# One plain weight pair instead of two in the second feed-forward block, two products moved between its halves, and part of the low-order rests formed by GpSimd

## The chip, the cores and the metric

The kernel runs on one core of one Trainium2 chip. The metric is the device time of one launch in microseconds (us). The times given as "before" are the median of three runs; the profile is of one further execution. A core's engines are called here TensorE (PE in the profile, its weight loads PEld), VectorE (DVE), ScalarE (ACT), GpSimd (POOL) and SyncE (SP), which issues the DMAs.

## The reference

One encoder layer on x of 512 tokens by 1024 features, all in float32:

```python
def rmsnorm(x, g):
    y = x32 * lax.rsqrt(jnp.mean(x32 * x32, axis=-1, keepdims=True) + EPS)
    return (y * g).astype(x.dtype)

def swiglu(x, w_in, w_out):                    # w_in 1024 x 5632, w_out 2816 x 1024
    gate, up = jnp.split(x @ w_in, 2, axis=-1)
    return (jax.nn.silu(gate) * up) @ w_out

h = swiglu(rmsnorm(x, norm_ffn1_pre), w_ffn1_in, w_ffn1_out)
x = x + 0.5 * rmsnorm(h, norm_ffn1_post)
h = mixer(rmsnorm(x, norm_mix_pre), ...)       # gated convolution and mLSTM heads, not touched by the change
x = x + rmsnorm(h, norm_mix_post)
h = swiglu(rmsnorm(x, norm_ffn2_pre), w_ffn2_in, w_ffn2_out)
x = x + 0.5 * rmsnorm(h, norm_ffn2_post)
```

The two swiglu blocks ("block 1" and "block 2") are what the change touches.

## The kernel before, in words

**Numbers in two parts.** TensorE works on a rounded form of float32 (F32R). To keep float32 accuracy each operand is split in two: `split(hi, lo, src)` lets ScalarE copy `src` rounded into `hi` (a CAST, L292) and then lets another engine subtract, `lo = src - hi` (a TENSOR_TENSOR, L294). The second part is called the rest here. Its engine is the argument `eng`, VectorE by default. Each product is then three matmul groups, hi x hi, hi x rest, rest x hi. In the names, `whi`/`wlo` are the two parts of a weight, `big` a tile of x, of a left matrix or of the hidden h, `raw` a weight as loaded by DMA, `ps` a PSUM bank.

**A feed-forward block** (`ffn`) makes the 2816 hidden features in 22 pairs of weight tiles (a gate tile and an up tile of 1024 x 128 each). The 512 tokens are taken as two halves of 256.

- *Plain pairs* (`PLAIN = 2`, `plain`, L453): the first two pairs are multiplied directly, first all four tiles with the first half of the tokens, then all four with the second half. The second half needs the transposes of tile 3 of the normalised x (`flip_q(3, ...)`, L343), which in block 2 hang on the last step of the mixer's output: `between` puts them into the fourth tile's first half, before its last third. Their results are split into xq tiles.
- *Split pairs* (the other 20; `product`, `mm_part`, L431): gate and up are computed together by a seven-product scheme (of Strassen's kind, as a 2 x 2 by 2 x 2 product: features halved, tokens halved), each product 12 matmuls of 128x256. The combinations of x (T1 to T4) are formed once per block in `combine_x`; those of the weights in `w_pair`, which forms four sums and differences on VectorE (L158) and splits g, s1, c and u. Products 1 and 2 need the first token half only; all others need the second half or T1 to T4. VectorE then joins the products (L484 to L509), from PSUM.
- *The output product* takes h (features by tokens) times w_out. Ten of the 22 feature tiles, in five pairs, go through the same scheme in two passes: five a-steps (`left_a`, `w_out_a`: products 1, 5, 6, 7) and, after the sums of these are taken out of PSUM (`taken`, L574 and L576 on ScalarE, L531 on VectorE), five b-steps (`left_b`, `w_out_b`: products 2, 3, 4), all L564; the other features go directly (`mm_out`, L589). `left_a` splits three parts of the left matrix (256, 256 and 512 columns), `w_out_a` splits a tile of 1024 and two halves of 512, `w_out_b` one of 1024 and one of 512, into a tile called `wt`.

**Order.** Weights come by SyncE's DMA queue in the order of `stream`, through four `raw` buffers; split weights have twelve `w` buffers. The order of instructions on each engine is set at build time by a scheduler that works with its own estimates of duration; instructions passed to `pin` stay in program order, as long as `pinned` says so, and all others may move. Each engine then runs its queue strictly in that order. GpSimd forms the rests of the first four weight tiles of the kernel only (`ON_POOL`), beside small work of the norms (L310), masks and memsets.

Of the kernel before, what the change touches and what calls it, by code (L numbers as in the profile page):

```python
# [19 lines left out]
NT = S // P  # L20
KD = D // P
DFF = 2816
NF = DFF // P
# [7 lines left out]
WARM = 20  # L31
WARM2 = 4
ON_POOL = (0, 1, 2, 3)
PLAIN = 2


@with_exitstack
def encoder_kernel(ctx: ExitStack, tc: tile.TileContext, a: dict, out: bass.AP):
    nc = tc.nc
# [73 lines left out]
    for w_in, w_out in ((w1i, w1o), (w2i, w2o)):  # L113
        if w_in is w2i:
            stream += [cols(wm, c) for c in (Q0, Q0 + P, K0, K0 + P)]
            stream += [cols(wm, O0 + i * P) for i in range(4)]
            stream += [cols(wm, CG)]
            stream += [(wm[blk(i, 2 * P), V0:V0 + 512].rearrange("(k p) f -> p k f", p=P), 2) for i in range(4)]
            for i in range(4):
                stream += [cols(wm, c + i * P) for c in ((CG, HC, BG) if i else (HC, BG))]  # L120
            stream += [rows(wo, k * P) for k in MIXK[:5]]
        for j in range(NF):
            pair = [cols(w_in, j * P), cols(w_in, DFF + j * P)]
            stream += pair if j < PLAIN else [([v[0] for v in pair], KD)]
# [26 lines left out]
    def w_pair(g, u):  # L151
# [34 lines left out]
    def w_out_a(r0, r1):  # L186

        c = (slice(0, 512), slice(512, 1024))

        def sub(o, a_, b_):  # L190
            nc.vector.tensor_tensor(out=o, in0=a_, in1=b_, op=ALU.subtract)

        def wt(n):
            return wpool.tile([P, 1024], F32R, tag="w", name=nm(n))

        sub(r1[:, c[0]], r0[:, c[1]], r0[:, c[0]])
        sub(r0[:, c[1]], r1[:, c[1]], r0[:, c[1]])
# [156 lines left out]
    def combine_x(xq):  # L354
# [5 lines left out]
        def sub(o, a_, b_):  # L360
            nc.vector.tensor_tensor(out=o, in0=a_, in1=b_, op=ALU.subtract)

        def put(key, v):
            hi, lo = xq_hl(xq, key)
            split(hi, lo, v)

        v1, v3 = (t4().rearrange("p (k t) -> p k t", k=4) for _ in range(2))
        sub(v1, b12, b11)
# [1 line left out]
        sub(v3, b22, b12)  # L370
        sub(b22, b22, v1)
        put("t2", b22)
        put("t3", v3)
        sub(b21, b21, b22)
        put("t4", b21)

    def pre_norm(tb, g, parts=2):
        xs = t4()
# [53 lines left out]
                    o, ww[:, k, :], x[xx][:, k, :], start=first and n == 0, stop=n == 11, skip_group_check=True))  # L432
                n += 1

    def ffn(xq, between, finish, mid=None, within=None, ahead=(2, 2, 1, 1), late=None):

# [25 lines left out]
        pinned["rest"] = False  # L462
        if late:
            with tc.issue_after(mark["hi"].ins), tc.issue_after(mark["lo"].ins):
                w_split(1)
# [7 lines left out]


        h0, h1 = slice(0, 256), slice(256, 512)
        right = {1: (0, 0), 2: (1, 0), 3: (1, 1), 4: "t4", 5: "t1", 6: "t2", 7: "t3"}

        def product(n, w, o, first):
            mm_part(o[:, h0], w[n], xq_hl(xq, right[n]), first)

        def last(j, w, x, c, u):
            product(4, w, x, False)
# [4 lines left out]
        for j in range(PLAIN, NF):  # L487
            if j == PLAIN + 4 and late:
                late()
            w = w_get(1 if j < NF - 1 else 2)  # L490
            x, y, z = ps(), ps(), ps()
            a_, u, c = t2(), t2(), t2()
            product(1, w, x, True)
            pinned["PE"] = False
            nc.scalar.copy(a_[:, h0], x[:, h0])
            product(5, w, y, True)
# [43 lines left out]
        def left_a(i):  # L540
# [181 lines left out]
    def within1(tb):  # L722
# [9 lines left out]
        finish1, wgates, within1, (1, 1, 1, 0), late1)  # L732
    xT = st["xT"]


# [393 lines left out]
    def store(tb, h):  # L1129
        nc.sync.dma_start(out[0, blk(tb), h], x_t[tb][:, h])  # L1130

    ffn(xT3, {(3, 2): lambda: flip_q(3, xs[3], xT3)}, lambda tb, acc: post_norm(tb, acc, g_post3, 4.0, store, (1, 0) if tb == NT - 1 else (0, 1)))


_INS = [
# [26 lines left out]
```

## Time and profile before

| | before |
|---|---|
| runs | 918.28 us median of 3 (918.09 to 918.73) |
| the profiled execution | 915.36 us, span of its instructions 913.7 us |
| granted TensorE clock | 0.999 of full speed |
| VectorE, rests of 128x1024 (L294) | 197 from weights, 1218 ns mean |
| ScalarE, casts of 128x1024 (L292) | 211, 1028 ns mean |
| GpSimd, rests of 128x1024 (L294) | 4, 2402 ns mean |
| DMA | 96.47 MB, 106 GB/s mean |

Block 1 has its plain pairs until 36 us, its split pairs until 244, its output product from 228 to 353 us; then comes the mixer. Block 2 starts at 567.6 us, has its split pairs until 798 and its output product from 783 to 907 us. Rows of the timeline give the start and the length of an instruction or of several alike (xN), the engine, the line, and in brackets how long the engine had been idle and what ended that. "Busy" counts time in which at least one instruction of an engine runs; consecutive instructions overlap by some tens of ns, so that work on an engine is better counted by the distance of starts. Lines of helpers stand for many callers: L294 is every rest.

### The profile page before, as it was taken

The numbers are of one execution on the slowest core, as the hardware profiler recorded it, in microseconds if no ns is written. First come the engines' busy times: TensorE is split into PE (matmuls) and PEld (weight loads), VectorE is DVE, ScalarE is ACT, GpSimd is POOL, SyncE is SP. The second block draws the span as 40 slices with busy tenths as digits, with TensorE's granted clock in tenths as the row PEclk, the third lists the DMA queues.
The fourth block names the chain that finished last, engine by engine and source line by source line (L and its number), as shares of the span: only waits on it lengthen the run. The fifth ranks groups of instructions, "written<-read, shape, count | busy, mean of one in ns | idle before, by whom it ended". The sixth has DMA issues, their size and how long they took to land.

```text
span 913.7 us, 15022 instructions
## 1 busy us (share of the span) xinstructions
PE 900.1 (99%) x6015; PEld 816.7 (89%) x6015; DVE 716.2 (78%) x1196; ACT 444.6 (49%) x745; POOL 44.7 (5%) x67
## 2 busy tenths in 40 slices
PE   8999999999999999999999999999999999999997
PEld 7999999999877888987888888999999999977885
DVE  6988998888988359498787746889888988999435
ACT  6655555555456235452434335545545545566311
POOL 5000000000002001000011000000000000000000
PEclk9999999999999999999999999999999999999999
DMA  8233443343335614231422602224343432343402
GB/s 256 68 114 116 119 135 97 102 127 96 93 127 149 199 47 116 63 100 47 116 70 70 197 12 66 74 68 118 112 120 93 118 108 87 119 140 110 162 2 91
DMA packets 126257, 96.47 MB, mean 106 GB/s; under 512 B 4182, under 2 KB 114794, under 8 KB 126187
## 3 DMA queue, kind: packets, MB, share of 16 engines
q1 hardware_dynamic: 126186, 95.51, 35.1%
q8 instruction: 47, 0.77, 0.4%
q14 instruction: 24, 0.19, 0.1%
HBM read 93.40 MB, written 2.10 MB: 105 GB/s over the span
## 4 chain that ended last, share of the span: by engine, by line
PE 93%; DVE 4%; ACT 1%; issue 1%; DMA 1%; SPq 0%; POOL 0%; DVEq 0%; POOLq 0%; ACTq 0%
PE ps L431 43%; PE ps L589 13%; PE ps L422 12%; PE ps L564 9%; PE ps L453 5%; PE ps L1119 5%; PE ps L965 2%; DVE big L294 1%; DVE wlo L294 1%; PE ps L343 1%; DVE big L531 1%; PE ps L1035 1%; DMA x<-in_x_dram 1%; PE ps L983 0%; PE ps L391 0%
## 5 line engine op out<-in xcount | busy, mean ns | idle before, releaser
L294 DVE TENSOR_TENSOR wlo<-raw,whi 128x1024 fp32r<-128x1024 f32 x207 | 245.0, 1192 | 58.9 <-ACT whi L292 44.2
L292 ACT CAST whi<-raw 128x1024 fp32r<-128x1024 f32 x211 | 211.8, 1028 | 145.9 <-DVE raw L158 45.0
L431 PE MATMUL ps<-big,whi 128*128 128x256 f32 x1920 | 264.8, 280 | 0.0
L431 PEld LDWEIGHTS ps<-big,whi 128*128 128x128 f32 x1920 | 243.5, 188 | 0.5
L431 PE MATMUL ps<-big,wlo 128*128 128x256 f32 x960 | 150.9, 280 | 0.0
L431 PEld LDWEIGHTS ps<-big,wlo 128*128 128x128 f32 x960 | 129.3, 188 | 0.0
L589 PE MATMUL ps<-whi,big 128*128 128x512 f32 x384 | 121.9, 395 | 0.2 <-ACT whi L292 0.2
L589 PEld LDWEIGHTS ps<-whi,big 128*128 128x128 f32 x384 | 72.0, 188 | 17.4 <-ACT whi L292 0.6
L422 PE MATMUL ps<-big,whi 128*128 128x512 f32 (+1 forms) x384 | 79.8, 358 | 0.2 <-DVE den L1053 0.2
L564 PE MATMUL ps<-whi,big 128*128 128x512 f32 x240 | 75.9, 395 | 2.6 <-ACT big L292 2.6
L589 PE MATMUL ps<-wlo,big 128*128 128x512 f32 x192 | 75.6, 395 | 0.0
L422 PEld LDWEIGHTS ps<-big,whi 128*128 128x128 f32 x384 | 63.5, 188 | 11.2 <-PE ps L1077 0.4
L431 PE MATMUL ps<-big,ws 128*128 128x256 f32 x480 | 65.3, 280 | 0.0
L431 PEld LDWEIGHTS ps<-big,ws 128*128 128x128 f32 x480 | 60.3, 188 | 0.0
L564 PEld LDWEIGHTS ps<-whi,big 128*128 128x128 f32 x240 | 44.7, 188 | 13.4 <-ACT big L292 3.4
L501 ACT COPY t<-ps 128x256 f32<-128x256 f32 x40 | 14.9, 371 | 72.8 <-PE ps L431 72.7
L292 ACT CAST big<-big 128x512 fp32r<-128x512 f32 (+2 forms) x68 | 36.1, 582 | 23.2 <-DVE big L531 10.8
L564 PE MATMUL ps<-wlo,big 128*128 128x512 f32 x120 | 44.9, 393 | 0.0
L589 PEld LDWEIGHTS ps<-wlo,big 128*128 128x128 f32 x192 | 36.1, 188 | 8.4
L422 PE MATMUL ps<-big,wlo 128*128 128x512 f32 (+1 forms) x192 | 41.1, 356 | 0.0
L294 DVE TENSOR_TENSOR big<-big,big 128x512 fp32r<-128x512 f32 (+2 forms) x68 | 40.7, 634 | 0.1
L422 PEld LDWEIGHTS ps<-big,wlo 128*128 128x128 f32 x192 | 32.1, 188 | 5.5
(212 smaller groups left out, 1143.3 us busy)
## 6 DMA issues: line engine op xcount, KB each, us to landing
raw<-in_w_ffn_in_dram SPq DMA_DIRECT2D x88, 512.0 KB, 4.8
raw<-in_w_ffn_out_dram SPq DMA_DIRECT2D x44, 512.0 KB, 5.0
raw<-in_w_mix_in_dram SPq DMA_DIRECT2D x24, 512.0 KB, 4.5
raw<-in_w_mix_out_dram SPq DMA_DIRECT2D x8, 512.0 KB, 3.6
raw<-in_w_ffn_out_dram SPq DMA_DIRECT2D x10, 256.0 KB, 4.0
out_dram<-x SPq DMA_DIRECT2D x8, 256.0 KB, 2.0
x<-in_x_dram SPq DMA_DIRECT2D x4, 256.0 KB, 4.9
x<-in_x_dram SPq DMA_DIRECT2D x2, 512.0 KB
```

Of the source, the lines that this page charges most:

```text
L292: latest["hi"] = nc.scalar.copy(out=hi, in_=src)
L294: latest["lo"] = eng.tensor_tensor(out=lo, in0=src, in1=f32(hi), op=ALU.subtract)
L343: pin(nc.tensor.transpose(out=pt[:, blk(k)], in_=xs[:, blk(4 * b + k)], identity=ident))
L422: nc.tensor.matmul(o, ww[:, k, :], xk(xT, xx, k, sl), start=n == 0, stop=n == 3 * KD - 1)
L431: pin(nc.tensor.matmul(o, ww[:, k, :], x[xx][:, k, :], start=first and n == 0, stop=n == 11, skip_group_check=True))
L453: pin(nc.tensor.matmul(o, ww[:, k, :], xq_hl(xq, (k // 4, th))[xx][:, k % 4, :], start=n == 0, stop=n == 3 * KD - 1))
L501: nc.scalar.copy(a_[:, h1], x[:, h0])
L531: nc.vector.tensor_tensor(out=o, in0=a_, in1=b_, op=op)
L564: nc.tensor.matmul(acc[tb + t][half], left[n][x][:, blk(t)], right[n][y], start=first and x == y == 0, stop=last_ and x == 1, skip_group_c ...
L589: nc.tensor.matmul(acc[tb][half], hT[hh][:, blk(tb)], w[ww][:, blk(half, 512)], start=fresh and hh == ww == 0, stop=k == NF - 1 and hh == ...
L965: nc.tensor.matmul(pv_, xk(xT, xx, k, blk(tb)), ww[:, k % 2, :], start=n == 0, stop=n == 3 * KD - 1)
L1119: nc.tensor.matmul(acc[half], yy[yi][:, k % 4, blk(tb)], wmo[k][wi][:, blk(half, 512)], start=(n == 0 and yi == 0 and wi == 0), stop=(n == ...
```

## The change

Three things. `PLAIN` becomes an argument of `ffn`: block 1 keeps two plain pairs, block 2 gets one, and its second pair becomes a split pair. In block 2 products 1 and 2 of the first split pair are issued between the two token halves of the plain pair, followed by the transposes of tile 3 (`fill`); the loop then leaves these two out for that pair. And several calls of `split` get `nc.gpsimd` as the engine of the rest, in both blocks: u in `w_pair`, two halves in `w_out_a`, one in `w_out_b`, the 512 columns in `left_a`, T3 and T4.

```diff
-PLAIN = 2
...
-            stream += pair if j < PLAIN else [([v[0] for v in pair], KD)]
+            stream += pair if j < (2 if w_in is w1i else 1) else [([v[0] for v in pair], KD)]
...
         uh, ul = wt("whi"), wt("wlo")
-        split(uh, ul, u)
+        split(uh, ul, u, nc.gpsimd)
...
-        split(bh[:, c[0]], bl[:, c[0]], r1[:, c[0]])
-        split(bh[:, c[1]], bl[:, c[1]], t)
+        split(bh[:, c[0]], bl[:, c[0]], r1[:, c[0]], nc.gpsimd)
+        split(bh[:, c[1]], bl[:, c[1]], t, nc.gpsimd)
...
-        split(t[:, c[0]], t[:, c[1]], r1[:, c[0]])
+        split(t[:, c[0]], t[:, c[1]], r1[:, c[0]], nc.gpsimd)
...
-        put("t3", v3)
+        put("t3", v3, nc.gpsimd)
         sub(b21, b21, b22)
-        put("t4", b21)
+        put("t4", b21, nc.gpsimd)
...
-    def ffn(xq, between, finish, mid=None, within=None, ahead=(2, 2, 1, 1), late=None):
+    def ffn(xq, between, finish, PLAIN, mid=None, within=None, ahead=(1, 1), late=None, fill=None):
...
+        pre = None
+        if fill:
+            pre = w_get(0), ps(), ps()
+            product(1, pre[0], pre[1], True)
+            product(2, pre[0], pre[2], True)
+            fill()
...
+            ready_ = pre if j == PLAIN else None
+            w = w_get(1 if j < NF - 1 else 2) if not ready_ else pre[0]
+            x, y, z = (pre[1], ps(), pre[2]) if ready_ else (ps(), ps(), ps())
...
+            if ready_:
+                w_split(1)
+            else:
+                product(1, w, x, True)
...
-            product(2, w, z, True)
+            if not ready_:
+                product(2, w, z, True)
...
-            split(hi[:, 512:1024], lo[:, 512:1024], a_)
+            split(hi[:, 512:1024], lo[:, 512:1024], a_, nc.gpsimd)
...
-    ffn(xT3, {(3, 2): lambda: flip_q(3, xs[3], xT3)}, lambda tb, acc: post_norm(...))
+    ffn(xT3, {}, lambda tb, acc: post_norm(...), 1, fill=lambda: flip_q(3, xs[3], xT3))
```

How this stands on the engines, at three places. First TensorE at the start of block 2 (numbers are tiles; L343/L342 are the transposes of tile 3, L453 matmuls of plain pairs, L431/L430 of split pairs; big_5654 and big_5663 are x's first token half, big_5848 and big_5856 its second). Before:

```order
L453 MATMUL ps_6027<-big_5654,whi_5949 128x256 x4
L453 MATMUL ps_6027<-big_5663,whi_5949 128x256 x4
L343 MATMUL ps_6044<-ident,t_875_5883 128x128 x4
L453 MATMUL ps_6027<-big_5654,wlo_5950 128x256 x2
L343 MATMUL ps_6051<-ident,t_875_5883 128x128 x4
L453 MATMUL ps_6027<-big_5654,wlo_5950 128x256 x2
L453 MATMUL ps_6027<-big_5663,wlo_5950 128x256 x4
L431 MATMUL ps_6212<-big_5654,whi_6010 128x256 x8
L431 MATMUL ps_6212<-big_5654,wlo_6011 128x256 x4
L453 MATMUL ps_5922<-big_5848,whi_5906 128x256 x4
```

and after:

```order
L453 MATMUL ps_5965<-big_5663,wlo_5913 128x256 x4
L430 MATMUL ps_5990<-big_5654,whi_5948 128x256 x8
L430 MATMUL ps_5990<-big_5654,wlo_5949 128x256 x4
L430 MATMUL ps_5991<-big_5663,whi_5948 128x256 x8
L430 MATMUL ps_5991<-big_5663,wlo_5949 128x256 x4
L342 MATMUL ps_6016<-ident,t_875_5883 128x128 x4
L342 MATMUL ps_6023<-ident,t_875_5883 128x128 x4
L453 MATMUL ps_5916<-big_5848,whi_5906 128x256 x4
L453 MATMUL ps_5965<-big_5848,whi_5912 128x256 x4
L453 MATMUL ps_5916<-big_5856,whi_5906 128x256 x4
```

Both products now stand ahead of the transposes, and the second token half (big_5848) follows directly behind them, where eighteen matmuls of the first half and of product 1 stood between.

Second, GpSimd's queue in block 2. Before, the small steps of the norms (rs) of block 2's input and output follow each other directly:

```order
L310 TENSOR_TENSOR rs_5878<-rs_5876,nhalf 128x1
L310 TENSOR_TENSOR rs_5892<-rs_5890,nhalf 128x1
L310 TENSOR_TENSOR rs_9392<-rs_9390,nhalf 128x1
L310 TENSOR_TENSOR rs_9442<-rs_9440,nhalf 128x1
L310 TENSOR_TENSOR rs_9491<-rs_9489,nhalf 128x1
```

After, 43 rests stand there; these are the first ones (u of the first split pair, T3, T4, u of the next two):

```order
L309 TENSOR_TENSOR rs_5878<-rs_5876,nhalf 128x1
L309 TENSOR_TENSOR rs_5892<-rs_5890,nhalf 128x1
L293 TENSOR_TENSOR wlo_5962<-raw_5943,whi_5961 128x1024
L293 TENSOR_TENSOR big_6067<-t_911_6057,big_6067 128x4x256
L293 TENSOR_TENSOR big_6071<-big_5666,big_6071 128x4x256
L293 TENSOR_TENSOR wlo_6126<-raw_6107,whi_6125 128x1024
L293 TENSOR_TENSOR wlo_6206<-raw_6187,whi_6205 128x1024
```

In the second block's order they are 21 rests of u, T3 and T4, then 10 weight halves, 5 left halves and 5 of `wt`; in block 1 the same with 20 of u. All come from VectorE's queue.

Third, ScalarE where the a-steps end and the first b-step begins (COPY rows are `taken`; big_8919, then big_8929, is the first b-step's left matrix). Before:

```order
L574 COPY big_8668<-ps_8660 128x512
L574 COPY big_8668<-ps_8661 128x512
L576 COPY big_8668<-ps_8662 128x512
L576 COPY big_8668<-ps_8663 128x512
L292 CAST wt_8879<-raw_8875 128x512
L292 CAST whi_8927<-raw_8925 128x1024
L292 CAST big_8919<-big_5898 128x512
```

and after:

```order
L586 COPY big_8678<-ps_8670 128x512
L291 CAST wt_8889<-raw_8885 128x512
L291 CAST whi_8937<-raw_8935 128x1024
L586 COPY big_8678<-ps_8671 128x512
L291 CAST whi_8943<-raw_8941 128x1024
L588 COPY big_8678<-ps_8672 128x512
L588 COPY big_8678<-ps_8673 128x512
L291 CAST big_8929<-big_5898 128x512
```

The two weight casts moved ahead of the last copies, so that the left matrix's cast now follows the copies directly.

More of the change, by code (lines that the diff above doesn't have):

```diff
@@ L361, in sub, with put @@
             nc.vector.tensor_tensor(out=o, in0=a_, in1=b_, op=ALU.subtract)
-        def put(key, v):
+        def put(key, v, eng=nc.vector):
             hi, lo = xq_hl(xq, key)
-            split(hi, lo, v)
+            split(hi, lo, v, eng)
         v1, v3 = (t4().rearrange("p (k t) -> p k t", k=4) for _ in range(2))
@@ L462, in ffn, with product @@
         pinned["rest"] = False
+        right = {1: (0, 0), 2: (1, 0), 3: (1, 1), 4: "t4", 5: "t1", 6: "t2", 7: "t3"}
+        def product(n, w, o, first):
+            mm_part(o[:, slice(0, 256)], w[n], xq_hl(xq, right[n]), first)
+        pre = None
[4 more added lines that the diff above has]
+            fill()
         if late:
@@ L475, in ffn @@
         h0, h1 = slice(0, 256), slice(256, 512)
-        right = {1: (0, 0), 2: (1, 0), 3: (1, 1), 4: "t4", 5: "t1", 6: "t2", 7: "t3"}
-        def product(n, w, o, first):
-            mm_part(o[:, h0], w[n], xq_hl(xq, right[n]), first)
         def last(j, w, x, c, u):
@@ L489, in ffn @@
                 late()
-            w = w_get(1 if j < NF - 1 else 2)
-            x, y, z = ps(), ps(), ps()
+            ready_ = pre if j == PLAIN else None
+            w = w_get(1 if j < NF - 1 else 2) if not ready_ else pre[0]
+            x, y, z = (pre[1], ps(), pre[2]) if ready_ else (ps(), ps(), ps())
             a_, u, c = t2(), t2(), t2()
-            product(1, w, x, True)
+            if ready_:
+                w_split(1)
+            else:
+                product(1, w, x, True)
             pinned["PE"] = False
@@ L731, in encoder_kernel @@
         },
-        finish1, wgates, within1, (1, 1, 1, 0), late1)
+        finish1, 2, wgates, within1, (1, 1, 1, 0), late1)
     xT = st["xT"]
@@ L1130, in store @@
         nc.sync.dma_start(out[0, blk(tb), h], x_t[tb][:, h])
-    ffn(xT3, {(3, 2): lambda: flip_q(3, xs[3], xT3)}, lambda tb, acc: post_norm(tb, acc, g_post3, 4.0, store, (1, 0) if tb == NT - 1 else (0, 1)))
+    ffn(
+        xT3, {}, lambda tb, acc: post_norm(tb, acc, g_post3, 4.0, store, (1, 0) if tb == NT - 1 else (0, 1)), 1,
+        fill=lambda: flip_q(3, xs[3], xT3),
+    )
 _INS = [
```

## The prediction

> **What bounds the kernel now.** I read the page's busy times first, then the chain of waits, then busy times by stage.
>
> ```profile
> PE 900.1 (99%) x6015; PEld 816.7 (89%) x6015; DVE 716.2 (78%) x1196; ACT 444.6 (49%) x745; POOL 44.7 (5%) x67
> PE 93%; DVE 4%; ACT 1%; issue 1%; DMA 1%; SPq 0%; POOL 0%; DVEq 0%; POOLq 0%; ACTq 0%
> ```
>
> TensorE is busy 99% of the span and the chain that ends last is 93% TensorE: time falls only if TensorE gets less to do or waits less, and it rises if anything makes TensorE wait. GpSimd is nearly free, which is what the change draws on. The next rows (PE, PEld, DVE, ACT, POOL busy) show where another engine stands close behind.
>
> ```profile
> 60.00:225.00 165.00, 165.00 (x1404) 165.00 (x1403) 143.09 (x224) 88.84 (x139) 0.00 (x0) 1.00 0.40 114
> 225.00:258.00 33.00, 33.00 (x182) 28.46 (x182) 33.00 (x66) 16.45 (x32) 0.00 (x0) 1.00 0.44 131
> 560.00:610.00 50.00, 50.00 (x400) 48.68 (x399) 42.12 (x60) 28.24 (x44) 2.01 (x3) 1.00 0.29 85
> 610.00:776.00 166.00, 166.00 (x1412) 166.00 (x1412) 143.34 (x225) 85.63 (x136) 0.00 (x0) 1.00 0.37 107
> 776.00:815.00 39.00, 39.00 (x224) 33.94 (x223) 38.27 (x72) 21.82 (x41) 0.00 (x0) 1.00 0.43 132
> 815.00:836.00 21.00, 18.62 (x78) 14.23 (x77) 19.88 (x34) 15.68 (x29) 0.00 (x0) 1.00 0.26 73
> ```
>
> In the split-pair stages (60:225, 610:776) TensorE never stops and VectorE is busy 86%: it has 14% to spare. Where the pairs end and the five a-steps of the output product run (225:258, 776:815), VectorE is busy 33.00 of 33.00 and 38.27 of 39.00 us beside a TensorE that does not stop either: two bounds at once. Right behind it (815:836) TensorE loses 2.4 us.
>
> **The change, part by part.** *One plain pair becomes a split pair in block 2.* A plain pair is 4 x 24 = 96 matmuls of 128x256, a split pair 7 x 12 = 84.
>
> ```profile
> 567.59 2.04 PE L453 MATMUL ps<-big,whi 128*128 128x256 f32 x16
> 577.93 0.60 PE L343 MATMUL ps<-ident,t 128*128 128x128 f32 x4
> 579.75 1.09 PE L431 MATMUL ps<-big,whi 128*128 128x256 f32 x8
> 581.13 2.50 PE L453 MATMUL ps<-big,whi 128*128 128x256 f32 x20
> 592.40 1.58 PE L431 MATMUL ps<-big,ws 128*128 128x256 f32 x12
> 593.82 1.11 PE L431 MATMUL ps<-big,whi 128*128 128x256 f32 x8
> 574.54 1.42 DVE L383 SCALAR_TENSOR_TENSOR t<-x,rs,gb 128x512 f32<-128x512 f32 x2 [0.44 <-POOL rs L310]
> 578.57 1.26 ACT L292 CAST big<-ps 128x512 fp32r<-128x512 f32 x2 [3.38 <-PE ps L343]
> ```
>
> The 12 matmuls at 592.40 take until 593.82, so 0.118 us each: 12 fewer are **-1.4 us** (a split period is 84 x 0.118 = 9.9 us).
>
> *Fill.* Tile 3 is ready at 574.54 + 1.42 = 575.96 and its transposes now come at 577.93, behind 88 matmuls. Afterwards 48 + 24 = 72 matmuls stand ahead of them: 567.59 + 72 x 0.118 = 576.1, still 0.1 us behind the data. But behind them one product (579.75 to 581.13) covers the ScalarE copies today; afterwards the second halves follow at once. The first copy ends 578.57 + 0.63 = 579.2, 1.27 us after the transposes began; the eight transposes cover about 0.8. That leaves 0.5; with the margin of 0.1 I take **+0.6** (0.4 to 1.3, if VectorE is late with tile 3).
>
> *The rests on GpSimd.* The order counts, per block, 20 or 21 rests of u (128x1024), T3 and T4 (128x1024), and in the output product 10 weight halves, 5 left halves and 5 of the fourth factor (128x512).
>
> ```profile
> L294 POOL TENSOR_TENSOR wlo<-raw,whi 128x1024 fp32r<-128x1024 f32 x4 | 9.6, 2402 | 1.4 <-ACT whi L292 1.3
> 777.67 2.36 DVE L294 TENSOR_TENSOR wlo<-raw,whi 128x1024 fp32r<-128x1024 f32 x2
> 779.94 0.42 DVE L508 TENSOR_TENSOR t<-ps,t 128x256 f32<-128x256 f32 x1
> 781.75 0.69 DVE L294 TENSOR_TENSOR wlo<-raw,whi 128x512 fp32r<-128x512 f32 x1
> 782.35 0.69 DVE L294 TENSOR_TENSOR wlo<-t,whi 128x512 fp32r<-128x512 f32 x1
> ```
>
> On VectorE one of 1024 takes (779.94 - 777.67)/2 = 1.13 us, one of 512 0.60 (781.75 to 782.35). On GpSimd one of 1024 takes 2.40; for 512 there is no row, half is 1.20, an estimate. If the two engines ran side by side, this would be free. The rows say that they do not:
>
> ```profile
> L706 POOL CAST big<-rawg x4: 209/440/1207, 284.0 to 285.4; 128x32 fp32r<-128x32 f32 x4
> 284.18 1.24 DVE L294 TENSOR_TENSOR wlo<-raw,whi 128x1024 fp32r<-128x1024 f32 x1 [0.26 <-ACT whi L292]
> 285.35 1.31 DVE L294 TENSOR_TENSOR big<-big,big 128x512 fp32r<-128x512 f32 x2
> 458.25 0.64 POOL L1018 TENSOR_SCALAR_AFFINE_SELECT t<-t 128x512 f32<-128x512 f32 x1 [14.08 <-ACT t L1016]
> 458.47 0.96 DVE L294 TENSOR_TENSOR big<-t,big 128x512 fp32r<-128x512 f32 x1
> ```
>
> The same little GpSimd cast takes 0.209 at best and 1.207 beside VectorE's subtraction of two SBUF operands at 284.18: it finishes when that one does. The other way round, the subtraction at 458.47 overlaps a GpSimd instruction for 0.42 us and takes 0.96 instead of 0.69: 0.27 lost, two thirds of the overlap. (The four GpSimd splits that give the 2.40 ran beside VectorE instructions that read PSUM, so they show nothing of this.) Nearly all that VectorE does in these stages reads two SBUF operands. So a rest on GpSimd costs VectorE between 0 and its whole length; the nearest row gives two thirds: 1.60 for 1024 against 1.13 saved, 0.80 for 512 against 0.60 saved. VectorE would lose by the move.
>
> Where this lands: per split pair VectorE has 0.86 x 9.9 = 8.5 us; 8.5 - 1.13 + 1.60 = 9.0 (9.8 at full length) of 9.9, so TensorE keeps setting the pace: **0** in steady pairs. At each block's start T3, T4 and the first u come within some 20 us on a loaded VectorE: 3 x 0.47 = 1.4 (0 to 3 x 1.27 = 3.8), partly absorbed: **+1** per block. Block 2 also gets a split pair's VectorE work, 8.5 us, in place of a plain pair's two splits and one product, 2 x 1.13 + 0.60 = 2.9; of the 5.6 more, T3, T4 and the first u (3.4) leave VectorE, and the 7.9 us that VectorE idles in 560:610 cover the rest; if that cover is gone, it adds up to 2.2. In the a-steps VectorE has no time to spare: 15 halves x 0.20 + one u of 0.47 = 3.5, and each rest comes 0.6 later (1.20 - 0.60) plus up to one instruction of 0.60 that holds GpSimd up, 4.7 together. How much TensorE feels depends on VectorE's lead.
>
> ```profile
> 813.46 0.68 DVE L294 TENSOR_TENSOR big<-big,big 128x512 fp32r<-128x512 f32 x1
> 813.84 0.86 PE L564 MATMUL ps<-wlo,big 128*128 128x512 f32 x3
> ```
>
> In block 2 the last left rest ends at 814.14 while TensorE is in the matmuls of that step: no lead, **+4**. For block 1 I take the middle, **+2**. Bounds: 0, or 15 x 0.60 + 1.27 = 10.3 if all of GpSimd's time blocks VectorE.
>
> VectorE's in-place differences in the left matrices now also wait for GpSimd, with all of VectorE's queue behind them; this is inside the same bounds. On the DMA queue nothing moves but one gain load; its loads wait for GpSimd instead of VectorE to free u, at most 2.4 us later, and the rest of u is needed by the last products of a pair only: nothing.
>
> *ScalarE's order at the first b-step.*
>
> ```profile
> 814.97 1.08 ACT L576 COPY big<-ps 128x512 f32<-128x512 f32 x2 [0.33 <-PE ps L564]
> 816.45 1.06 ACT L292 CAST whi<-raw 128x1024 fp32r<-128x1024 f32 x1
> 817.40 1.97 ACT L292 CAST big<-big 128x512 fp32r<-128x512 f32 x4
> 818.08 0.50 PE L564 MATMUL ps<-whi,big 128*128 128x512 f32 x1 [1.28 <-ACT big L292]
> 263.27 0.50 PE L564 MATMUL ps<-whi,big 128*128 128x512 f32 x1 [1.28 <-ACT big L292]
> ```
>
> TensorE waits 1.28 us in each block for a cast that stands behind two weight casts, which the new order puts ahead of the last copies. Closed in both blocks it is -2.6; if VectorE is late already, nothing. I take **-1.3**.
>
> Sum: -1.4 + 0.6 + 1 + 1 + 2 + 4 - 1.3 = +5.9. The profiled execution took 915.36 (span 913.7) and would take 921.3; it lies 2.9 under the median of the runs, 918.28, which becomes **924.2**.
>
> **Rivals.** *VectorE's lead is enough (faster).* For: 14% to spare in the pairs. Against: none to spare at 776:815. It decides if a rest on GpSimd blocks VectorE for less than it saves, under 1.13 of 2.40. Then -1.4 + 0.6 - 2.6 = -3.4: 914.9.
>
> *The terms cancel (no change):* the a-steps cost 1 to 3 in all, 917 to 920.
>
> *Full blocking.* Each GpSimd rest holds VectorE for its whole length: (10.3 - 2 of lead) + 10.3 in the a-steps, 2 at each start, no gap closed: -0.8 + 18.6 + 4 = +21.8, 940. For: the casts at 284 waited for all of VectorE's instruction. Against: the row at 458.47, two thirds. The Trainium skill (SBUF — State Buffer, "Who interferes with whom") states this rule: VectorE with two SBUF inputs and a GpSimd instruction that reads SBUF exclude each other, and the later one blocks until the other is done. By that rule the sum would be this rival's; the trace agrees for GpSimd waiting (1.207 against 0.209) and shows VectorE waiting only once.
>
> **Chances.** Forecast (920.2 to 932) 0.45, full blocking 0.15, faster 0.26, cancelled 0.14. The bound of what can be told from no change is 0.2%, 1.8 us: faster 0.26, same 0.14, slower 0.60. The range 914.0 to 939 leaves out the lower fringe of the faster case and the upper half of full blocking; the forecast's own is 920.2 to 932.
>
> **What would show it.** VectorE's subtractions of 1024 lengthen from 1.22 where GpSimd runs, and GpSimd's from 2.40; TensorE's new idle time is named after L564's successors waiting for POOL or DVE rests around 225:260 and 775:820; the 1.28 waits shrink; the transposes of tile 3 start near 576 with about half a microsecond of wait behind them. I am wrong if VectorE's instructions keep their lengths beside GpSimd, or if the a-steps run without gaps.

## The result and the profile after

| | before | after |
|---|---|---|
| runs | 918.18 us median of 4 (917.49 to 918.73) | 952.93 us median of 4 (947.38 to 954.66) |
| ratio | | 1.0368 (95% interval 1.0326 to 1.0411) |
| profiled execution | 915.36 us, span 913.7 | 952.85 us, span 951.1 |
| granted TensorE clock | 0.999 | 0.989 |

The change makes the kernel 3.7% slower, about 34 us; the prediction said 924.2 (914.0 to 939.0). The direction was right, the size was not.

The page after, busy times and the chain of waits:

```profile
PE 914.1 (96%) x6003; PEld 823.6 (87%) x6003; DVE 746.3 (78%) x1121; ACT 447.1 (47%) x750; POOL 240.0 (25%) x152
PE 24%; DVE 4%; POOL 2%; ACT 1%; issue 1%; DVEq 0%; POOLq 0%; ACTq 0%
```

VectorE has 75 instructions fewer and is busy 30 us longer. TensorE has 12 matmuls fewer and is busy 14 us longer: part of the loss is a slower clock. Before, 93% of the span could be followed through TensorE; now the chain passes to and fro between the engines.

Busy times by stage (stretch, length, then PE, PEld, DVE, ACT, POOL, granted clock, DMA share, GB/s): the steady pairs of both blocks, the a-steps of both, and the first b-steps of block 2.

```profile
93.00:232.00 139.00, 139.00 (x1183) 138.93 (x1182) 120.78 (x172) 72.96 (x114) 34.81 (x15) 1.00 0.36 106
240.00:275.00 35.00, 28.48 (x125) 22.32 (x124) 33.09 (x43) 14.63 (x27) 26.97 (x13) 0.95 0.32 104
660.00:800.00 140.00, 140.00 (x1193) 140.00 (x1192) 121.04 (x174) 73.11 (x114) 34.94 (x15) 1.00 0.36 104
807.00:842.00 35.00, 27.98 (x140) 22.16 (x139) 32.87 (x47) 14.95 (x26) 20.21 (x13) 1.00 0.27 85
842.00:875.00 33.00, 27.35 (x108) 21.55 (x107) 26.26 (x38) 20.17 (x35) 16.81 (x4) 0.90 0.30 100
```

The steady pairs still lose nothing, with GpSimd at work a quarter of the time. In the output product TensorE loses 5.7 to 7.0 us per 33 to 35 us; in the a-steps VectorE is nearly as full as before.

By places, from the starts of matmuls in the two profiled executions: block 1, from its first plain matmul to its last output matmul, takes 355.5 us instead of 341.6 (+13.9); the mixer the same within 0.3; block 2 360.7 instead of 339.5 (+21.2). Within the blocks, at the same matmul in both executions: ahead of the a-steps block 1 loses 6.1 us and block 2 7.3 (both in the first pairs, and block 2 has 12 matmuls fewer besides), in the a-steps 9.1 and 8.3, behind them block 1 gains 1.3 and block 2 loses 5.7. The rest, 2.1 us, lies ahead of block 1 and does not belong to the change: in the profiled execution of before the first transposes already ran at full clock (0.11 us apart), in that of after still at half (0.21). This is probably also most of the 2.8 us by which the profiled execution of before lies under its median.

The groups of VectorE and GpSimd (count, then busy us and mean ns of one), first two of before, then after:

```profile
L158 DVE TENSOR_TENSOR t<-raw 128x512 f32<-128x512 f32 x40 | 27.3, 684 | 6.8 <-DMA raw<-in_w_ffn_in_dram 6.7
L531 DVE TENSOR_TENSOR t<-big 128x256 f32<-128x256 f32 x10 | 4.1, 415 | 0.0
```

```profile
L157 DVE TENSOR_TENSOR t<-raw 128x512 f32<-128x512 f32 x41 | 49.1, 1198 | 0.1
L543 DVE TENSOR_TENSOR t<-big 128x256 f32<-128x256 f32 x10 | 8.1, 811 | 0.1
L293 DVE TENSOR_TENSOR wlo<-raw,whi 128x1024 fp32r<-128x1024 f32 x157 | 224.8, 1436 | 96.6 <-ACT whi L291 78.3 <-PE ps L601 9.2 <-PE ps L576 4.1
L514 DVE TENSOR_TENSOR t<-ps,t 128x256 f32<-128x256 f32 x41 | 17.1, 417 | 7.9 <-PE ps L430 7.8
L293 POOL TENSOR_TENSOR wlo<-raw,whi 128x1024 fp32r<-128x1024 f32 x45 | 113.5, 2523 | 294.5 <-ACT whi L291 191.5 <-PE ps L430 59.8 <-DVE wlo L293 35.2
L293 POOL TENSOR_TENSOR wt<-raw,wt 128x512 fp32r<-128x512 f32 x10 | 25.4, 2538 | 39.2 <-ACT wt L291 39.2
L293 POOL TENSOR_TENSOR big<-big,big 128x512 fp32r<-128x512 f32 x10 | 23.8, 2389 | 21.4 <-ACT big L291 21.4
```

VectorE instructions with two SBUF operands lengthen where they meet a GpSimd rest, the same work from 684 to 1198 and from 415 to 811; one that reads PSUM (L514) stays at 417. GpSimd's rests of 512 columns of the fourth factors (wt) and the left matrices (big) take 2.4 to 2.5 us on average, twice the estimate of 1.20; those of the weight halves take 1.5 to 1.6.

How both happen is seen in block 2. Rows of the timeline:

```profile
831.84 1.47 POOL L293 TENSOR_TENSOR wlo<-raw,whi 128x512 fp32r<-128x512 f32 x1
833.28 1.44 POOL L293 TENSOR_TENSOR wlo<-t,whi 128x512 fp32r<-128x512 f32 x1
833.52 2.28 DVE L293 TENSOR_TENSOR wlo<-raw,whi 128x1024 fp32r<-128x1024 f32 x1
835.85 0.50 PE L576 MATMUL ps<-wlo,big 128*128 128x512 f32 x1 [2.56 <-DVE wlo L293]
845.91 1.30 POOL L293 TENSOR_TENSOR wt<-raw,wt 128x512 fp32r<-128x512 f32 x1 [2.55 <-ACT wt L291]
854.39 12.78 POOL L293 TENSOR_TENSOR wt<-raw,wt 128x512 fp32r<-128x512 f32 x1 [7.18 <-ACT wt L291]
856.06 2.83 DVE L293 TENSOR_TENSOR big<-big,big 128x512 fp32r<-128x512 f32 x5
867.22 2.50 PE L576 MATMUL ps<-wt,big 128*128 128x512 f32 x5 [4.49 <-POOL wt L293]
869.95 0.63 PE L601 MATMUL ps<-wlo,big 128*128 128x512 f32 x1
873.76 0.39 PE L601 MATMUL ps<-wlo,big 128*128 128x512 f32 x1
```

At 833.52 VectorE's subtraction of 1024 meets a GpSimd rest that runs until 834.72, and ends 1.08 us after that, at 835.80, where 1.22 is its length by the profile when nothing is in its way: it did next to nothing until GpSimd was done. In this execution 82 VectorE instructions with two SBUF operands start during a GpSimd rest and come out more than 0.1 us longer; each of them loses the whole of its overlap but 0.13 to 0.14 us. TensorE waits 2.56 us for the one at 833.52. At 854.39 it is the other way round: VectorE has subtraction after subtraction (none of them slowed), and a GpSimd rest like the one of 1.30 us at 845.91 takes 12.78; TensorE, which needs it, waits 4.49 us. In the 11.53 us in which GpSimd didn't get in, VectorE had no pause (columns as above):

```profile
854.52:866.05 11.53, 8.21 (x36) 6.32 (x34) 11.53 (x20) 5.68 (x10) 11.53 (x1) 0.97 0.00 1
```

GpSimd isn't always kept out like this. The rest at 833.28 took 1.44 us: VectorE's instruction before it had itself been held by GpSimd, and GpSimd got in ahead of VectorE's next one. Behind the wait of 4.49 us the matmuls come at half speed: the five at 867.22 start 0.46 us apart on average instead of 0.23, and single ones last 0.63 until 872, 0.39 afterwards.

### The profile page after: what moved, and what is told of

Same layout as the page of the kernel before. It is cut to its first block, busy times and chain, and to the rows that moved or that the text cites. A ratio compares the mean times of both kernels' runs of the same rounds, so it can differ in the third digit from the quotient of the medians.

```text
span 951.1 us, 15244 instructions
## 1 busy us (share of the span) xinstructions
PE 914.1 (96%) x6003; PEld 823.6 (87%) x6003; DVE 746.3 (78%) x1121; ACT 447.1 (47%) x750; POOL 240.0 (25%) x152
## 5 line engine op out<-in xcount | busy, mean ns | idle before, releaser
L291 ACT CAST whi<-raw 128x1024 fp32r<-128x1024 f32 (+1 forms) x212 | 213.4, 1029 | 194.9 <-DVE raw L157 84.8
L293 DVE TENSOR_TENSOR wlo<-raw,whi 128x1024 fp32r<-128x1024 f32 x157 | 224.8, 1436 | 96.6 <-ACT whi L291 78.3
L430 PE MATMUL ps<-big,whi 128*128 128x256 f32 x1968 | 275.5, 282 | 7.1 <-DVE t L520 2.6
L430 PEld LDWEIGHTS ps<-big,whi 128*128 128x128 f32 x1968 | 251.3, 190 | 10.1 <-DVE t L520 3.6
L293 POOL TENSOR_TENSOR wlo<-raw,whi 128x1024 fp32r<-128x1024 f32 (+1 forms) x55 | 128.9, 2345 | 301.8 <-ACT whi L291 194.1
L430 PE MATMUL ps<-big,wlo 128*128 128x256 f32 x984 | 156.2, 282 | 0.0
L430 PEld LDWEIGHTS ps<-big,wlo 128*128 128x128 f32 x984 | 133.9, 190 | 0.2 <-DVE wlo L293 0.2
L601 PEld LDWEIGHTS ps<-whi,big 128*128 128x128 f32 x384 | 72.8, 190 | 17.4
L421 PEld LDWEIGHTS ps<-big,whi 128*128 128x128 f32 x384 | 63.4, 188 | 11.3 <-PE ps L1089 0.4
L430 PE MATMUL ps<-big,ws 128*128 128x256 f32 x492 | 67.4, 280 | 0.0
L430 PEld LDWEIGHTS ps<-big,ws 128*128 128x128 f32 x492 | 62.0, 188 | 0.0
L309 POOL TENSOR_TENSOR rs<-rs,nhalf 128x1 f32<-128x1 f32 x24 | 13.6, 567 | 187.3 <-DVE rs L305 178.5
L157 DVE TENSOR_TENSOR t<-raw 128x512 f32<-128x512 f32 x41 | 49.1, 1198 | 0.1
L518 ACT ACTIVATE t<-t 128x512 f32<-128x512 f32 x41 | 25.9, 631 | 40.1 <-DVE t L514 38.4
```

The costliest lines, as they stand in the source:

```text
L157: nc.vector.tensor_tensor(out=o, in0=a_, in1=b_, op=op)
L291: latest["hi"] = nc.scalar.copy(out=hi, in_=src)
L293: latest["lo"] = eng.tensor_tensor(out=lo, in0=src, in1=f32(hi), op=ALU.subtract)
L309: nc.gpsimd.tensor_tensor(out=r[:, 0:w], in0=acc, in1=nhalf[:, 0:w], op=ALU.pow)
L421: nc.tensor.matmul(o, ww[:, k, :], xk(xT, xx, k, sl), start=n == 0, stop=n == 3 * KD - 1)
L430: pin(nc.tensor.matmul(o, ww[:, k, :], x[xx][:, k, :], start=first and n == 0, stop=n == 11, skip_group_check=True))
```

## The experiments

Medians and ratios are against the kernel before, run beside them on the same chip (its median 917.4 to 917.9); a ratio of 1.001 is 0.9 us. The theory: *the two engines exclude each other*, so a rest on GpSimd holds VectorE for its whole length, and TensorE feels it where VectorE has no lead. The rivals: the change of the pairs costs the time; or what costs is the later arrival of a rest made by a slower engine.

| run | median us | ratio (95% interval) |
|---|---|---|
| pair change alone | 920.49 | 1.0035 (1.0024 to 1.0047) |
| all rests, no pair change | 945.89 | 1.0345 (1.0304 to 1.0386) |
| output-product rests alone | 938.26 | 1.0226 (1.0204 to 1.0247) |
| u's rest alone | 922.93 | 1.0062 (1.0043 to 1.0082) |
| T3 and T4 alone | 918.96 | 1.0018 (1.0005 to 1.0031) |
| dummy subtractions | 945.74 | 1.0307 (1.0291 to 1.0323) |
| dummy writes, three fills | 934.65 | 1.0183 (1.0168 to 1.0198) |
| dummy writes, two fills | 926.69 | 1.0105 (1.0086 to 1.0124) |
| fills of the rest's tile | 921.18 | 1.0042 (1.0025 to 1.0058) |
| fill and subtraction of the rest's tile | 946.08 | 1.0320 (1.0299 to 1.0342) |
| left casts first | 919.09 | 1.0018 (1.0008 to 1.0027) |
| cast order | 914.03 | 0.9967 (0.9956 to 0.9978) |
| pair change, T parts by ScalarE | 918.10 | 1.0014 (1.0004 to 1.0023) |

### The parts of the change

*Pair change alone*: all `nc.gpsimd` arguments taken back.

```diff
-        split(uh, ul, u, nc.gpsimd)
+        split(uh, ul, u)
...
-            split(hi[:, 512:1024], lo[:, 512:1024], a_, nc.gpsimd)
+            split(hi[:, 512:1024], lo[:, 512:1024], a_)
```

> All rests back on VectorE; only block 2's second pair as a split pair, its two early products and the transposes behind them are left of the change. Blocking theory (GpSimd's rests hold VectorE's subtractions and so cost the time): the whole loss goes, -1 to +3 us against the kernel before (-1.4 for 12 matmuls, +0.6 for the fill, up to +2.2 for the split pair's VectorE work), TensorE's clock stays at 0.999. Rival, the pair change costs it: block 2 keeps most of its 21 us, +10 to +20.

It costs 0.35%, just above the range of the theory and far from the rival. Where: TensorE waits for VectorE between 594 and 650 us, and VectorE for loads. Rows of its timeline, then of its chain of waits (start, us, what):

```profile
615.50 0.69 DVE L157 TENSOR_TENSOR t<-raw 128x512 f32<-128x512 f32 x1 [2.15 <-DMA raw<-in_w_ffn_in_dram]
617.78 1.20 PE L430 MATMUL ps<-big,whi 128*128 128x256 f32 x8 [1.44 <-DVE t L520]
```

```profile
609.54 1.14 DVE wlo L293
610.70 4.77 DMA raw<-in_w_ffn_in_dram
...
620.06 1.13 DVE wlo L293
621.22 4.93 DMA raw<-in_w_ffn_in_dram
...
630.40 1.13 DVE wlo L293
631.56 4.86 DMA raw<-in_w_ffn_in_dram
```

A loop: a late rest frees a `raw` buffer late, the load into it (4.8 us) starts late, VectorE waits for it and is late again. It turns in 10.3 to 10.5 us (610.70, 621.22, 631.56) against 9.9 for TensorE's pair.

*All rests without the pair change*, and its parts (the `nc.gpsimd` arguments of the change put into the kernel before, all of them; those of `w_out_a`, `w_out_b` and `left_a`; that of u; those of T3 and T4):

> The kernel before with all the GpSimd rests of the change and no change of pairs. Blocking theory: +33 to +37 us, block 1 exactly as in the changed kernel (+16), block 2 within 3 us of its +21. Rival, the pair change costs block 2's part: about +16 to +22 in all.

> The kernel before with only the output product's rests on GpSimd (25 of 128x512 per block: w_out_a, w_out_b, left_a). Blocking theory, each held for the whole GpSimd instruction of 1.2 to 1.5 us against 0.60 saved: TensorE gaps in the a- and b-steps only, +8 us in block 1 and +14 in block 2, together +18 to +24; nothing before 228 us. Rival, the losses come from the block starts and a late VectorE carries them into the output product: under +8.

> The kernel before with only u's rest (128x1024, one per split pair) on GpSimd. Blocking theory: VectorE loses 2.4 and saves 1.13 per pair, 8.5 + 1.3 = 9.8 of 9.9 us: steady pairs keep 9.9 us; starts and the last pair lose a little: +2 to +8. Rival, VectorE's lead covers u wholly: within 1 us of the kernel before.

> The kernel before with only T3's and T4's rests (128x1024, once each per block) on GpSimd. If the parts add up, this is what rests-only has beyond output-only and u-only: 31.7 - 20.5 - 5.2 = +6, at 38 to 50 us and 590 to 620 us. Blocking alone: each holds VectorE 2.4 to 3.7 us against 1.13 saved, so +1.3 to +2.6 for each, +2.5 to +5 per block if VectorE has no lead there, less 1 to 2 for the lead: +2 to +8. Rival, these two are harmless and the 6 is an interaction with u's rest: within 1 us of before.

(The output product's rests on GpSimd are 20 per block, not 25 as written there.) Two came out under what was expected: all rests cost 31.7 us by the ratio, not 33 to 37, and T3 and T4 1.7 us, not 2 to 8. The rests make nearly the whole loss, the pair change a tenth. The output product has 2.3% of it, split evenly (block 1 +10.6, block 2 +10.3 in the profiled executions, nearly all of it behind 230 us); u 0.6%, T3 and T4 0.2%. The three parts sum to 3.06%, all rests together cost 3.45%: a little may be interaction, within the intervals. If so, it sits at the block starts: in the profiled executions, one of each, the two blocks lose about 11 us ahead of the a-steps with all rests, 4 with u's rest alone and 1.5 with T3 and T4 alone. In u's run the steady pairs again lose nothing; it loses at 72, 84, 618 and 628 us, just behind the block starts, and half a microsecond more at the first b-step of block 1.

### Held or late?

*Dummy subtractions*: VectorE keeps its rests, GpSimd does the same subtraction beside it into a scratch tile. *Dummy writes*: one column is read, then the scratch tile is filled.

```diff
+    def dummy(hi, src):
+        pin(nc.gpsimd.tensor_tensor(out=scratch, in0=src, in1=f32(hi), op=ALU.subtract))
...
+        dummy(bh[:, c[0]], r1[:, c[0]])
         split(bh[:, c[0]], bl[:, c[0]], r1[:, c[0]])
```

```diff
+    def dummy(hi, src):
+        pin(nc.gpsimd.tensor_copy(scratch[:, 0:1], f32(hi)[:, 0:1]))
+        for _ in range(3):
+            pin(nc.gpsimd.memset(scratch, 0.0))
```

> The kernel before, all rests on VectorE as they were; beside each of the 40 output-product rests that the change moved, GpSimd does the same subtraction once more into a scratch tile that nobody reads. No rest comes later by its own length, so only the hold on VectorE can cost. Blocking theory: VectorE's subtractions of two SBUF operands lengthen by a whole GpSimd instruction where they meet, VectorE gets no work off, so the loss is as large as output-only's +20.5 or larger, +20 to +45. Rival, the loss is the rest's own later arrival (GpSimd 1.5 to 2.5 us against 0.6): +0 to +6, VectorE's lengths unchanged.

> As the dummy subtractions, but GpSimd copies one column of the cast part (so that it comes at the same time) and then fills the scratch tile three times (128x512 memsets, about 0.5 us each): GpSimd just as long at work, but nearly no reads of SBUF. Blocking theory, only reads collide: VectorE's 128x512 subtractions stay at 0.68 us and the time within 2 us of before. Rival, any GpSimd work beside VectorE costs: at least half of what the dummy subtractions cost.

> As the dummy writes, with two fills in place of three at each of the 40 places. In the kernel with three, VectorE's lengths stayed (128x512 rests 0.69, 128x1024 1.22), yet ScalarE waited for GpSimd, 9.3 us in block 1's output product alone (the longest 5.1): GpSimd's queue of 1.9 to 2.0 us per place ran behind and held the cast parts' buffers. If that backlog was the whole cost, 1.2 us per place (an unblocked rest's length) keeps up: VectorE's lengths again unchanged, ScalarE no longer waits for GpSimd, +0 to +4 us. Rival, GpSimd's work costs by itself: +10 or more.

The subtractions that nobody reads cost 3.1%, more than the real move of the same rests (2.3%), as the theory had it. They too hold a tile until GpSimd has read it, but little time is lost in that way: ScalarE waits 0.6 us for them to let go of a buffer and VectorE 3.7. The writes did not behave as expected: VectorE's lengths stayed (its 128x512 rests, 681 before), yet 1.8% was lost, through ScalarE, which waited for GpSimd to let go of buffers (waits in 225:290: total, times, longest):

```profile
L298 DVE TENSOR_TENSOR big<-big,big 128x512 fp32r<-128x512 f32 x44 | 29.5, 693 | 12.4 <-ACT big L296 12.3
```

```profile
ACT big L296 <- POOL scratch L302: 9.3, 2, 5.1
```

With two fills I expected these waits to go; they did not (12.9 us in four). Two rows of that run's timeline, GpSimd's copy that held a buffer and TensorE's wait for the cast behind it:

```profile
807.94 13.02 POOL L302 CAST scratch<-big 128x1 bf16<-128x1 f32 x1
825.96 0.50 PE L574 MATMUL ps<-whi,big 128*128 128x512 f32 x1 [3.31 <-ACT big L296]
```

A GpSimd copy of a single column, 0.19 us when undisturbed, took 13.02: VectorE had two-operand subtractions without a pause from 807.94 to 820.92, as the third busy time of this line says (12.97 of 12.98 us), and GpSimd read only when VectorE stopped.

```profile
807.94:820.92 12.98, 12.98 (x58) 10.51 (x57) 12.97 (x22) 7.29 (x13) 12.98 (x1) 1.00 0.49 156
```

So these two runs do not separate reads from writes, since reading one column is enough to be kept out. The next pair does.

*Fills of the rest's own tile*, three writes, or one write and one subtraction of the tile from itself, ahead of the same 40 rests:

```diff
+    def dummy(lo):
+        for _ in range(3):
+            pin(nc.gpsimd.memset(f32(lo), 0.0))
...
+        dummy(bl[:, c[0]])
         split(bh[:, c[0]], bl[:, c[0]], r1[:, c[0]])
```

```diff
+    def dummy(lo):
+        pin(nc.gpsimd.memset(f32(lo), 0.0))
+        pin(nc.gpsimd.tensor_tensor(out=lo, in0=f32(lo), in1=f32(lo), op=ALU.subtract))
```

> The kernel before; ahead of each of the 40 output-product rests GpSimd fills the rest's own tile (the low part) three times (memsets of 128x512, 1.6 us together), as soon as its buffer is free; VectorE then writes the rest over it. No reads, and no buffer of the cast part held. Blocking theory: VectorE's lengths unchanged, +0 to +5 (where VectorE waits for a late fill). Rival, any GpSimd work costs: as the next one.

> The same tile, the same places, but one fill and then one GpSimd subtraction of the tile from itself (128x512, reads SBUF; about 0.5 + 1.2 us unblocked, as long as three fills). The one difference to the three fills is that it reads. Blocking theory: VectorE's subtractions lengthen beside it, GpSimd's subtraction waits for VectorE in turn (over 1.5 us), and the time rises by +10 us or more above the three fills. Rival, the length of GpSimd's work alone counts: within 4 us of the three fills.

Groups of the fills, then of the fill with subtraction:

```profile
L302 POOL MEMSET wt<- 128x512 f32 x30 | 15.8, 528 | 50.4 <-PE ps L572 45.6 <-ACT whi L295 3.6
L297 DVE TENSOR_TENSOR big<-big,big 128x512 fp32r<-128x512 f32 x44 | 29.2, 689 | 0.0
```

```profile
L302 POOL TENSOR_TENSOR wt<-wt 128x512 fp32r<-128x512 f32 x10 | 36.4, 3643 | 0.8
L297 DVE TENSOR_TENSOR big<-big,big 128x512 fp32r<-128x512 f32 x44 | 35.8, 836 | 0.0
```

and of the latter's waits:

```profile
PE ps L572 <- DVE wlo L297: 7.8, 5, 3.0
```

Writes alone: 0.4%, no length changes. With the read: 3.2%, GpSimd's subtractions of wt take 3.6 us on average, VectorE's from 689 to 836, and TensorE's largest wait is for VectorE's rests. Same places, same tile; the difference of 2.8%, 25 us, is the read. VectorE's busy time says the same: 716.0 us with writes alone (716.2 before), 745.0 with the read, while VectorE waited only 2.8 us for GpSimd to be done with a tile. This shows the exclusion. It does not say that lateness costs nothing: in the output-product run TensorE waits 7.3 us directly for rests made by GpSimd (wlo, wt and big, in 225:300 and 780:870), and 6.2 for VectorE; these rests were late because GpSimd was kept out, the other face of the same exclusion.

### The order of casts

The prediction's last term said that TensorE's 1.28 us waits come from a weight cast standing ahead of the left casts. *Left casts first* turns the two round in both blocks; *cast order* also puts the next steps' fourth factors ahead of the left and h casts that stood in front of them.

```diff
-                left, right = left_b(n), w_get(2)
+                left = left_b(n)
+                if n == 0:
+                    with tc.issue_after(latest["hi"].ins):
+                        right = w_get(2)
+                else:
+                    right = w_get(2)
```

```diff
+                    with tc.issue_after(fourth[f0 + n - 1][0].ins), tc.issue_after(fourth[f0 + n - 1][1].ins):
+                        left = left_b(n)
```

> The kernel before with one order changed: at the first b-step of both blocks ScalarE casts the left parts ahead of the 128x1024 weight cast that stood in front of them. If that cast is what TensorE's 1.28 us waits at 263.27 and 818.08 are made of, each shrinks by its 0.95 to 1.06: -1.9 to -2.1 in all (915.8). Rival, another operand of the step is as late (VectorE's rest of the left part or the weight rest behind it): within 0.5 us of before.

> The kernel before with the left casts of the first b-step ahead of the weight cast (as in cast-first), and besides, the fourth factor's cast and rest of a step ahead of the left and h casts of the next ones. In cast-first the waits at the first b-step fell from 1.44 to 0.50 each, but the wait for the fourth factor's cast at the second step rose (block 2: 1.05 to 1.71, and TensorE's clock halved behind it). If that was where the gain went, both now go: -2 to -4 us, about 914 to 916. Rival, the work of ScalarE and VectorE here is itself the bound and the wait moves on to the next step: within 1 us of before.

The first: the waits at the first b-step fell from 1.44 to 0.50 each, as expected, but the time rose by 0.2%. At the second b-step of block 2 TensorE, now earlier, waits longer for the fourth factor (0.88 before; its timeline):

```profile
835.14 0.50 PE L564 MATMUL ps<-wt,big 128*128 128x512 f32 x1 [1.55 <-ACT wt L292]
```

and then, in this execution, loses 1.6 us to a halved clock. Only four of the twelve runs have a mean clock as low as this one's (0.996), so part of the rise stays unexplained. The second order takes that wait away; all that is left of waits in the output products is

```profile
PE ps L566 <- ACT big L294: 0.7, 2, 0.3
```

It takes 0.33% less than the kernel before, so it is faster than both kernels: the 4.4 us of waits (over 0.3 us each) that TensorE had in the output products were a matter of queue order.

### The pair change once more

*T parts by ScalarE*: as the pair change alone, with the second parts of T1 to T4 taken off VectorE. ScalarE writes a second cast in their place, so this kernel leaves out four subtractions per block and does not compute the layer; it only has the same TensorE work.

```diff
-            split(hi, lo, v, eng)
+            pin(nc.scalar.copy(out=hi, in_=v))
+            pin(nc.scalar.copy(out=lo, in_=v))
```

> The pair change alone, as in pair-only, but T1's to T4's second parts are written by ScalarE (a second cast, so the second parts are not rests and the sums are not those of the reference) instead of VectorE: 4 x 1.13 = 4.5 us less for VectorE at each block's start, the same TensorE work. If the pair change's 3.3 us above the kernel before (4.7 above its own -1.4) come from VectorE being late by the extra split pair, which frees the raw buffers late, so that the weight loads come late for the next pairs (TensorE waits at 594, 616, 628 and 649 us), then most of those 3.5 us go: 916 to 918.5, and VectorE no longer waits 2.15 us for a load near 615. Rival, the second half's transposes and the early products are the cost: it stays at 919.5 to 921.

2.0 of the 2.8 us between the medians go; the waits from 594 to 650 us are gone, while a single one of 1.4 us for ScalarE, which has more to do, stands at 589. TensorE's loss in 585:652, first the pair change alone, then this:

```profile
585.00:652.00 67.00, 63.97 (x533) 62.95 (x533) 57.59 (x90) 35.82 (x56) 0.00 (x0) 1.00 0.28 80
```

```profile
585.00:652.00 67.00, 65.55 (x557) 65.35 (x556) 57.03 (x92) 40.45 (x63) 0.00 (x0) 1.00 0.34 98
```

So VectorE's lateness is the cause of most of the cost. VectorE waited for loads in this run too (3.9 us in four waits, the longest 1.4), so the loop through the `raw` buffers is read from the chain and not broken by this experiment alone.

## Why the prediction was wrong, step by step

- *Fewer matmuls, -1.4.* Right: 6003 for 6015.
- *Fill, +0.6.* Right by itself: in the pair change alone TensorE waits 0.44 and 0.41 behind the transposes, 0.85 in all (bounds 0.4 to 1.3). With the rests on GpSimd it is 0.46 + 1.45, the second for VectorE's rests of tile 3.
- *The pair's VectorE work, covered by 7.9 us of idle time.* Wrong: the whole pair change came to +0.35% instead of -0.8 us. The cover was named, but VectorE's idle time there is time in which data is not yet there; work that comes earlier in the queue delays buffers and loads, and these come back as waits. The bound of 2.2 was too small: 3.5 us were lost at 594 to 650.
- *Steady pairs, 0.* Right: 139.00 of 139.00 and 140.00 of 140.00 us.
- *Block starts, +1 each.* Far too small: ahead of the a-steps block 1 loses 6.1 us and block 2, with the pair change, 7.3 where the sum had 0.2. T3 and T4 alone cost 0.18% in both blocks, near enough; but u's rests, of which the sum counted the first one only, cost 0.62% alone, and all of them together more than their parts. In the kernel after, block 1's start loses 4.3 us in five waits between 42 and 78 us and 1.7 to the clock.
- *The a-steps, +2 and +4.* This term and the block starts are the steps that failed most. The a-steps cost 9.1 and 8.3 us in the kernel after. With the output product's rests alone, block 1 loses 10.6 and block 2 10.3, of which 8.7 and 7.2 lie in the a-steps. Two inputs were wrong. First, the share for which a GpSimd rest holds VectorE: I took two thirds from one row (458.47, where 0.27 of 0.42 was lost). It is the whole overlap less a fixed 0.14 us, as 833.52 and the 81 other instructions show. The row at 458.47 says this too (0.42 - 0.27 = 0.15): I read a fixed piece as a share, and carried it from an overlap of 0.42 to rests of 1.2 and 2.4 us. The other row, GpSimd's 1.207 us, had said "all". Second, the length of a GpSimd rest: 1.20 is near an undisturbed one (1.30), but where VectorE is full it waits up to 12.78 us. The prediction let GpSimd be kept out for one VectorE instruction of 0.60 at most.
- *The b-steps, nothing but the cast order.* Wrong in block 2: 5.7 us are lost behind the a-steps, with the largest single wait of the kernel, 4.49 us, for a rest on GpSimd, and the halved clock behind it. The sum left the GpSimd rests of the b-steps out without a reason.
- *Cast order, -1.3.* Right in size, by luck in the way it came about: TensorE's idle time ahead of the first b-step went from 1.28 to 0.11 us in block 1 and from 1.28 to 1.16 in block 2. The sum had taken the middle between both gaps closed and none. The experiments show that another order nearly closes both.
- *Not in the sum at all:* TensorE's clock, four stretches at half speed, 7.6 us together (contained in the figures by place).

The rival "full blocking", 940, had the right mechanism and gave 13 us too little. In the profiled executions its 18.6 for the a-steps is near the 17.4 measured. What it lacks is the block starts with the pair change, 13.4 us where it counted 3.2, and block 2's loss behind the a-steps. The Trainium skill states it (SBUF — State Buffer, "Who interferes with whom"): two SBUF inputs on VectorE contend with a GpSimd instruction that reads SBUF, not with one that only writes it, and issue order decides which of them is blocked. The fills with and without a read agree with the first, 1.0320 against 1.0042; with the second the trace agrees at 833.52 but not at 854.39, where nineteen VectorE instructions that began after the GpSimd rest went ahead of it, and the measurement decides. I gave a measured row the word against it, and had read that row wrong.

In the profiled executions the 37.4 us between the spans are, by kind: 2.1 start, -1.4 matmuls, 7.6 at the halved clock, 26.9 of new waits over 0.3 us (31.3 against 4.4 before in the two blocks, from the starts of matmuls), and 2.2 that is left, in shorter waits.

## What to carry to other kernels

Work moved from VectorE to GpSimd isn't moved off VectorE where VectorE reads two operands from SBUF and GpSimd reads SBUF too: count it at its GpSimd length on VectorE wherever the two meet, and count as well that GpSimd may not get in until VectorE pauses. Idle time of an engine covers new work only if it isn't itself a wait for data; follow which buffers the work frees. When a kernel sits at 99% of TensorE, look for the last microseconds in the queue order of the casts, and check the step after the one you mend.

## What was not expected of the hardware

- *GpSimd can be kept out for many VectorE instructions with two SBUF operands, not only for one:* 12.78 us for a 128x512 subtraction, 13.02 us for a copy of 128x1, both until VectorE paused. A rest at 240.29 in the kernel after took 3.51 us and got in when VectorE came to an instruction that reads PSUM; the one at 833.28 got in directly behind a VectorE instruction that GpSimd had held. What decides between these isn't shown.
- *TensorE's clock halves after a fixed stretch of 3.41 us in which TensorE stood still for about 2 us in all.* In the kernel after, the granted clock is at half from 46.13, 267.99, 646.87 and 865.33 us, for 3.41 us, the last time for 6.83. These starts are 65, 111 and 64 times 3.413 us apart: they lie on one grid. Five cells of that grid (columns as above, the granted clock is the third figure from the end):

```profile
244.10:247.51 3.41, 2.17 (x10) 1.42 (x8) 3.41 (x4) 1.05 (x1) 3.41 (x3) 1.00 0.51 202
247.51:250.93 3.42, 1.61 (x7) 1.36 (x8) 3.42 (x8) 0.77 (x2) 0.80 (x1) 1.00 0.01 5
250.93:254.34 3.41, 3.41 (x17) 2.75 (x16) 3.41 (x8) 1.94 (x4) 2.07 (x1) 1.00 0.14 31
264.58:267.99 3.41, 1.56 (x8) 0.94 (x7) 2.71 (x3) 0.20 (x2) 3.41 (x4) 1.00 0.35 136
267.99:271.41 3.42, 3.42 (x10) 2.65 (x9) 3.42 (x3) 2.04 (x3) 3.42 (x2) 0.50 0.58 157
```

Counted from the starts of matmuls, TensorE stood still for 2.2 us in the cell at 264.58, and the next one ran at half clock. The longer wait that ended at 249.32 fell into two cells, 1.4 us into the first and 1.8 into the second, and the clock stayed. The traces of all fifteen kernels agree, from 16 us on and outside the slow stretches themselves: each of 36 cells with more than 2.08 us of idle time was followed by one at half clock (15 of them at the end of a kernel), none of 3912 with less than 1.9 us was, and of the seven between, four. A cell at half clock costs 1.7 us of matmul time, so a wait of 2 us costs 2 or 3.7, as it falls on the grid. The Trainium skill (TensorE: Matmul & The Clock Gate, "Part 1: The HAM clock gate (the "warmup" mystery)") names an idle window of about 3.4 us, which runs freely, as the condition. The grid and the length of the stretches agree with such a window; that about 2 us of idle time in it were enough doesn't, and here the measurement decides.
